# Memory attention and mLSTM numerators: from fp32 matrix products to three rounded products of split operands

## The chip, the cores and the metric

The kernel runs on one core of a Trainium2 chip. The metric is the device time of one execution in microseconds, the median of several runs. A core has TensorE (PE, matrix products; its weight loads are shown apart as PEld), VectorE (DVE), ScalarE (ACT), GpSimd (POOL) and SyncE (SP, which here issues the weight transfers).

## What is computed

A decoder trunk of two layers on 256 tokens of width 1024. Each layer is a half-step SwiGLU feed-forward (hidden width 2816), a token mixer beside four heads of attention to a memory of 256 rows, and a second half-step feed-forward. The mixer of layer 0 (mixer A) is an mLSTM with four heads, that of layer 1 (mixer B) banded attention with sixteen heads. All inputs are float32. What the change touches:

```
mem_kv = rms_norm(mem, mem_norm_g) @ mem_w_kv            # keys: first 512 columns, values: last 512
# memory_heads, per layer and head (dimension 128):
q = rms_norm(xq, q_norm_g); k = rms_norm(mem_k, k_norm_g)
s = einsum('bthd,bmhd->bhtm', q, k) * M_HD ** -0.5
p = softmax(s);  o = einsum('bhtm,bmhd->bthd', p, mem_v)
# mLSTM, per head (q, k of 128, v of 256):
s = einsum('bhjd,bhsd->bhjs', qc, kc) * exp(log_d - m_t[..., None])
num = einsum('bhjs,bhsv->bhjv', s, vc) + (part of the earlier chunks)
den = sum(s) + ...;  h = num / max(|den|, exp(-m_t))
```

The kernel computes the mLSTM over all 256 tokens at once: a lower triangle of score tiles d (128x128 tiles: three per head) times v. A column of ones next to v's 256 columns gives the denominators.

## The kernel before

**Split operands.** Nearly all products are "rounded": a float32 matrix is split into a high half, rounded to float32r, and a low half, the rest. `mm3` adds three products of the halves (low x high, high x high, high x low). Weights come in by DMA (`wr`), ScalarE writes the high half (`wh`), VectorE the low half (`wl`). Activations are split likewise (`xh`, `xl`; in the general pool tiles named `u`). `split_plain` splits as it stands, `split_gain` multiplies by a column first: both take one ScalarE and one VectorE instruction. In a product one side moves through TensorE and one stands in it; the profile names the moving one first. In the feed-forwards and output projections the weights stand; in the projections by rows (memory keys and values, memory queries, mLSTM v, all of mixer B's input) the weights move and the activations stand.

**Products that are fp32.** `mmf` issues a plain float32 product, which the profile shows as two MATMUL records. It is used for the memory scores (`kT` moving, query `qT` standing), the memory values (`pT` moving, `vM` standing), the mLSTM scores and the mLSTM numerators (`v` moving with 257 columns, score tiles `d` standing). Transpositions (with the identity `con`) and mixer B's banded attention are fp32 as well.

**Side chains.** The main program issues the large projections. Each head is a chain of steps started beside it: for a memory head queries, scores, softmax, transposition of p, values; for an mLSTM head scores, numerators, normalisation, transposition. The steps are `cross_spawn` and its inner `queries` and `head`, and `scores` and `numerators` in `mixer_a`.

**Order.** The kernel is first recorded, then `plan` orders all instructions on each engine with a table of durations: TensorE takes the next run of the main program or a side run whose operands are ready; VectorE and ScalarE take the instruction that is due first; SyncE issues transfers in the recorded sequence. A rule with `HOLD` holds back a lone side run for up to 2 us while the previous product was a rounded one, so that side runs come together. Tiles come from pools with a fixed number of buffers: `up` (31 units of 2 KB a partition), `tp` (7 of the same size, named `t`), `vp` (2), `whp` and `wlp` (8 each), `cp` (small columns).

**Addresses.** In the built program the activation halves (pools `xhp`, `xlp`, `up`) begin at byte 448 modulo 512 of a partition, and the weight halves (`whp`, `wlp`) and `tp` at 0. `kT` and `vM` are at 448, `v` at 448 and 480.

Of the kernel before, what the change touches and what calls it, by code (L numbers as in the profile page):

```python
# [10 lines left out]
F32 = mybir.dt.float32  # L11
# [8 lines left out]
P = 128  # L20
# [153 lines left out]
class Slot:  # L174
    def __init__(self, pool, tag, number, shape, dt, name):
        self.key, self.pool, self.number, self.uses, self.made = (pool.name, tag), pool, number, [], None
        self.args = (shape, dt, tag, name)

    def real(self):
        if self.made is None:  # L180
# [144 lines left out]
def plan(rec):  # L325
# [11 lines left out]
    tiles_of, touched = [[] for _ in ops], [[] for _ in ops]  # L337
    for slots in rec.slots.values():
        over = []
        for s in slots:  # L340
            s.users = sorted({u[0].n for u in s.uses})
            s.first, s.left, s.end, s.free_from, s.psum = s.users[0], len(s.users), 0.0, 0.0, s.key[1] == "bank"
# [100 lines left out]
    while remaining:  # L443
        found = []
        if now:
            found.append((free["tensor"], now[0], None))
        else:
            t0 = free["tensor"]
            head = main[at["main"]] if at["main"] < len(main) else None
            r0 = ready(head[0]) if head else None  # L450
            if head and tiles_of[head[0].n] and side and len(places[tiles_of[head[0].n][0].key]) <= SPARE:
                r0 = None
            best, there = None, 0
            for run in side[:24]:
                r = run_ready(run)
                if r is not None:
                    r += MARGIN
                    there += r <= t0
                    if best is None or max(r, t0) < best[0]:
                        best = (max(r, t0), run, r)  # L460
            if best and last_kind and there < 2 and t0 - best[2] < HOLD and r0 is not None and r0 <= t0:
                best = None
            if best and (r0 is None or best[0] <= max(r0, t0)):
                found.append((best[0], best[1][0], best[1]))
            elif r0 is not None:
                found.append((max(r0, t0), head[0], head))
# [68 lines left out]
def tile_trunk(ctx: ExitStack, nc, a, out):  # L535
# [15 lines left out]
    xhp = pool("xhp", 4)  # L551
    xlp = pool("xlp", 4)
    up = pool("up", 31)
    vp = pool("vp", 2)
    wrp = pool("wrp", 5)
    whp = pool("whp", 8)
    wlp = pool("wlp", 8)
    tp = pool("tp", 7)
    sp = pool("sp", 2)
    ap1 = pool("ap1", 1)  # L560
    gp = pool("gp", 1)
# [10 lines left out]
    def unit(dt):  # L572
        return mk(up, [P, 2, T], dt, "u")

    def tmp():
        return mk(tp, [P, 2, T], F32, "t")

    def col():
        return mk(cp, [P, 16], F32, "col")
# [267 lines left out]
        return halves(ps)  # L847


    kT = [mk(cst, [P, 2, T], F32, f"kT{i}") for i in range(2)]  # L850
    vM = mk(cst, [P, 2, 512], F32, "vM")
    x0 = Norm(G_F1)

    def memory():
# [20 lines left out]
        norm = Norm(G_MEM, rows=False)  # L875

        def keys(gi, kr):
            nc.scalar.copy(kT[gi], turn(kr))
            return
            yield  # L880

# [13 lines left out]
        def finish(raw):  # L895
            for c2 in range(4):
                norm.square(memT[c2], c2 == 0)
                yield 2.0
            norm.fold()
            yield LAT['mnorm']  # L900
            yield from norm.chain()
            yield LAT['mrest']
            for h in range(2):
                nc.vector.tensor_scalar(vM[:, h], vM[:, h], norm.rc[:, h:h + 1], None, op0=ALU.mult)
            hsc = head_scales(norm.zc, P, False)
            for i in range(2):
# [5 lines left out]
        raw = [unit(F32) for _ in range(2)]  # L912
        for gi in range(4):
            gr = Group(wkv, gi * 256, mh, ml, rows=True)
            wts = [wcols(wkv, 768, kh) for kh in range(2)] if gi == 3 else wfirst if gi == 0 else [None] * 2
            if gi == 3:
                for c2 in range(4):
                    x0.put(xT[c2], False)
            for kh in range(2):
                if gi == 0 and kh == 0:  # L920
                    yield from gr.first_part(wts[0])
                else:
                    yield from gr.part(kh, wts[kh])
            dst = raw[gi] if gi < 2 else vM[:, :, (gi - 2) * 256:(gi - 1) * 256]
            wv.spawn(late(dst, gr), LAT['raw'])
# [108 lines left out]
    def cross_spawn(gr, gi, layer, hsc, ys):  # L1034
# [4 lines left out]

        def queries():  # L1040
            ps = turn(qn)
            qT = unit(F32)
            act(qT, ps, AF.Copy, scale=gqk[:, layer:layer + 1])
            cell.append(qT)
            for m in range(2):
                wv.spawn(head(m), LAT['cross_s'] + LAT['cross_m'] * m)
            return
            yield

        def head(m):  # L1050
            hd, qT = gi * 2 + m, cell[0]
            hi, lo = ys.tiles(4 + gi)
            s = mo()
            for h in range(2):
                mmf(s[:, h * T:(h + 1) * T], qT[:, m, h * P:(h + 1) * P], kT[gi][:, m], T)
            sv = halves(s)
            c = col()
            nc.vector.tensor_reduce(out=c[:, 0:2], in_=sv, axis=AX.X, op=ALU.max, negate=True)
# [9 lines left out]
            for mc in range(2):  # L1068
                for h in range(2):
                    transpose(tps[:, mc * T + h * P:mc * T + (h + 1) * P], p[:, h, mc * P:(mc + 1) * P])  # L1070
            pT = tmp()
            nc.scalar.copy(pT, halves(tps))
            yield LAT['cross_o']
            o = mo()
            for mc in range(2):
                mmf(o[:, :T], vM[:, mc, hd * P:(hd + 1) * P], pT[:, mc], T, mc == 0, mc == 1)
            split_plain(o[:, :T], hi[:, m], lo[:, m])
            ys.done.add(8 + hd)

# [38 lines left out]
    def mixer_a(x, nxt):  # L1118
# [112 lines left out]

        def numerators(hd, v):
            d = sd[hd]
            nps = [mo(), mo()]
            mmf(nps[0][:, :257], d[:, :P], v[:, 0, :257], 257)
            mmf(nps[1][:, :257], d[:, P:T], v[:, 0, :257], 257, True, False)
            mmf(nps[1][:, :257], d[:, T:384], v[:, 1, :257], 257, False, True)
            c, junk = col(), tmp()
            for h in range(2):
                nc.vector.tensor_copy(c[:, h:h + 1], nps[h][:, T:T + 1])  # L1240
# [35 lines left out]
    rope_s = mk(cst, [P, 2, 2, ROT], F32, "rope_s")  # L1276

    def rope_tables():
        w16 = [mk(sp, [P, 2, 8], F32, f"rope{i}") for i in range(5)]
        ang, k, r, sn, cs = w16  # L1280
        posf = col()
        nc.vector.tensor_copy(posf[:, 0:2], posi)
# [216 lines left out]
```

## Time and profile before

| | |
|---|---|
| three runs | 998.93 us (median), 998.85 to 999.69 |
| the profiled execution | 998.74 us |
| its span | 997.0 us |
| granted TensorE clock | 1.0 |
| TensorE, VectorE, ScalarE busy | 99%, 67%, 53% |
| instructions | 20571, 8560 of them MATMUL records |

The span is divided as follows (us from its start): memory stage to about 31, first feed-forward to about 237, mixer A to about 324, two feed-forwards to about 709, mixer B to about 813, last feed-forward to the end. Every operation is issued by one helper, so all have one line (237); groups are told apart by the names of their tiles.

### The profile page before, as it was taken

Reading aid. Unit: us, or ns where it says so; the run is one execution under the profiler, and the core shown is the slowest. Engines: PE = TensorE matmul, PEld = TensorE weight load, DVE = VectorE, ACT = ScalarE, POOL = GpSimd, SP = SyncE. Lnnn points to the kernel's source line nnn. Section 1 sums busy time; section 2 is a strip of 40 time slices with the busy share of each in tenths; the row PEclk is TensorE's granted clock in tenths of the full one; section 3 lists DMA queues with packets and bytes.
Section 4 is the critical chain, followed back from the end, with each engine's and each line's share of the span. In section 5 each row is a group of like instructions: output and inputs, shape, how many; then the busy total and the mean of one; then the engine's idle time right before and its main releaser. Section 6 shows DMA issues by size and latency. Waiting matters only on the chain.

```text
span 997.0 us, 20571 instructions
## 1 busy us (share of the span) xinstructions
PE 990.9 (99%) x8560; PEld 974.1 (98%) x8560; DVE 664.6 (67%) x1080; ACT 532.8 (53%) x779; POOL 27.0 (3%) x27
## 2 busy tenths in 40 slices
PE   9999999999999999999999999999999999999998
PEld 7999999999999999999999999999998899999998
DVE  6986665578756686666567766656677777666552
ACT  7764545446746554444455544445578765544440
POOL 0020000000001000000000000000113000000000
PEclk9999999999999999999999999999999999999999
DMA  9966665667544566665666666556633437665550
GB/s 323 299 200 193 195 189 179 198 171 206 155 149 148 170 212 192 195 200 173 190 202 204 192 196 198 176 187 200 184 106 123 132 106 235 195 199 187 181 169 22
DMA packets 173204, 182.70 MB, mean 183 GB/s; under 512 B 7124, under 2 KB 168328, under 8 KB 173112
## 3 DMA queue, kind: packets, MB, share of 16 engines
q1 hardware_dynamic: 171872, 179.60, 58.6%
q10 hardware_dynamic: 1016, 1.58, 0.5%
q8 instruction: 67, 1.10, 0.5%
q0 software_dynamic: 224, 0.22, 0.2%
q14 instruction: 25, 0.20, 0.1%
HBM read 180.32 MB, written 1.05 MB: 182 GB/s over the span
## 4 chain that ended last, share of the span: by engine, by line
PE 98%; DMA 1%; SPq 0%; DVE 0%; ACT 0%; issue 0%
PE bank L237 98%; DMA wr<-in_mem_w_kv_dram 1%; SPq L237 0%; DVE wl L237 0%; ACT wh L237 0%; DVE t L237 0%
## 5 line engine op out<-in xcount | busy, mean ns | idle before, releaser
L237 DVE TENSOR_TENSOR wl<-wr,wh 128x1024 fp32r<-128x1024 f32 (+1 forms) x349 | 414.8, 1191 | 265.2 <-ACT wh L237 263.6
L237 ACT CAST wh<-wr 128x1024 fp32r<-128x1024 f32 (+1 forms) x349 | 357.8, 1027 | 390.2 <-PE bank L237 372.9
L237 PE MATMUL bank<-xh,wh 128*128 128x256 f32 x1544 | 427.0, 277 | 0.0
L237 PE MATMUL bank<-xh,wl 128*128 128x256 f32 x1544 | 426.7, 276 | 0.0
L237 PE MATMUL bank<-xl,wh 128*128 128x256 f32 x1544 | 426.5, 276 | 0.0
L237 PE MATMUL bank<-u,wh 128*128 128x256 f32 x1792 | 307.3, 277 | 0.0
L237 PEld LDWEIGHTS bank<-xh,wh 128*128 128x128 f32 x1544 | 290.0, 188 | 0.1
L237 PEld LDWEIGHTS bank<-xh,wl 128*128 128x128 f32 x1544 | 290.0, 188 | 0.0
L237 PEld LDWEIGHTS bank<-xl,wh 128*128 128x128 f32 x1544 | 289.9, 188 | 0.1
L237 PEld LDWEIGHTS bank<-u,wh 128*128 128x128 f32 x1792 | 270.0, 188 | 1.4 <-issue 1.4
L237 PE MATMUL bank<-u,wl 128*128 128x256 f32 x896 | 248.1, 277 | 0.0
L237 PEld LDWEIGHTS bank<-u,wl 128*128 128x128 f32 x896 | 168.3, 188 | 0.5 <-issue 0.5
L237 PE MATMUL bank<-wh,xh 128*128 128x256 f32 x208 | 58.6, 282 | 0.0
L237 PE MATMUL bank<-wh,xl 128*128 128x256 f32 x208 | 58.6, 282 | 0.0
L237 PE MATMUL bank<-wl,xh 128*128 128x256 f32 x208 | 58.3, 280 | 0.0
L237 DVE TENSOR_TENSOR t<-bank,rb 128x256 f32<-128x256 f32 x88 | 36.6, 421 | 11.1 <-PE bank L237 9.1
L237 DVE TENSOR_TENSOR u<-t,u 128x512 fp32r<-128x512 f32 (+1 forms) x59 | 40.4, 685 | 0.3
L237 PEld LDWEIGHTS bank<-wh,xh 128*128 128x128 f32 x208 | 39.1, 188 | 0.1
L237 PEld LDWEIGHTS bank<-wh,xl 128*128 128x128 f32 x208 | 39.0, 188 | 0.1
L237 PEld LDWEIGHTS bank<-wl,xh 128*128 128x128 f32 x208 | 39.0, 188 | 0.1
L237 DVE TENSOR_TENSOR t<-t,bank 128x256 f32<-128x256 f32 x88 | 32.8, 414 | 1.1 <-ACT t L237 1.1
L237 POOL TENSOR_TENSOR col<-col,mhalf 128x4 f32<-128x4 f32 (+2 forms) x15 | 21.8, 1456 | 294.1 <-DVE col L237 294.1
(134 smaller groups left out, 581.5 us busy)
## 6 DMA issues: line engine op xcount, KB each, us to landing
wr<-in_ffn_w_in_dram SPq DMA_DIRECT2D x176, 512.0 KB, 4.4
wr<-in_ffn_w_out_dram SPq DMA_DIRECT2D x80, 512.0 KB, 4.2
wr<-in_a_w_in_dram SPq DMA_DIRECT2D x28, 512.0 KB, 3.7
wr<-in_b_w_in_dram SPq DMA_DIRECT2D x14, 512.0 KB, 4.5
wr<-in_a_w_out_dram SPq DMA_DIRECT2D x12, 512.0 KB, 3.3
wr<-in_b_w_out_dram SPq DMA_DIRECT2D x12, 512.0 KB, 3.5
wr<-in_ffn_w_out_dram SPq DMA_DIRECT2D x16, 256.0 KB, 2.8
wr<-in_mem_w_kv_dram SPq DMA_DIRECT2D x7, 512.0 KB, 7.7
```

The lines of the kernel that those rows point to most:

```text
L237: getattr(getattr(nc, op.engine), op.kind)(*map(real, op.args), **{k: real(x) for k, x in op.kw.items()})
```

## The change

The products of the memory heads and of the numerators become three rounded products each. Keys and values of the memory are kept as high and low halves: 2 x 2 tiles `kT`, two tiles `vM`. The values go through two more `u` units first and are scaled and split by `split_gain`. The query becomes two `t` tiles, the transposed probabilities two `u` tiles, the mLSTM score tiles two `t` tiles, and v two tiles with 258 columns (the ones column and a second one; zeros in the low half). Scores keep kT moving and the query standing; values keep the probabilities moving and vM standing; numerators keep v moving and the score tiles standing.

Gaps in the constants and between the two v pools set addresses: `kT` at 448, `vM` at 0, the v halves at 448 and 480, all modulo 512; the pools behind keep the offsets that they had modulo 512. `tp` grows to 8, the rope tables' small tiles come from `cp`, and the area for GpSimd's transfer descriptors is halved. In `plan` the `HOLD` rule no longer holds a side run that begins with a rounded product. The mLSTM scores, the transpositions and mixer B's banded attention stay as they were.

```diff
-            if best and last_kind and there < 2 and t0 - best[2] < HOLD and r0 is not None and r0 <= t0:
+            if best and last_kind and not best[1][0].rounded and there < 2 and t0 - best[2] < HOLD and r0 is not None and r0 <= t0:
...
-    vp = pool("vp", 2)
+    vhp = pool("vhp", 2)
+    gap = pool("gap", 1)
+    vlp = pool("vlp", 2)
...
-    tp = pool("tp", 7)
+    tp = pool("tp", 8)
...
-    kT = [mk(cst, [P, 2, T], F32, f"kT{i}") for i in range(2)]
-    vM = mk(cst, [P, 2, 512], F32, "vM")
+    kT = [[mk(cst, [P, 2, T], F32R, f"kT{i}{j}") for j in range(2)] for i in range(2)]
+    mk(cst, [P, 16], F32, "gap1")
+    vM = [mk(cst, [P, 2, 512], F32R, f"vM{j}") for j in range(2)]
+    mk(cst, [P, 112], F32, "gap2")
+    mk(gap, [P, 112], F32, "gap")
...
         def keys(gi, kr):
-            nc.scalar.copy(kT[gi], turn(kr))
+            split_plain(turn(kr), *kT[gi])
...
-            for h in range(2):
-                nc.vector.tensor_scalar(vM[:, h], vM[:, h], norm.rc[:, h:h + 1], None, op0=ALU.mult)
+            for i in range(2):
+                for h in range(2):
+                    split_gain(raw[2 + i][:, h], norm.rc[:, h:h + 1],
+                               *(v[:, h, i * 256:(i + 1) * 256] for v in vM))
...
         def queries():
             ps = turn(qn)
-            qT = unit(F32)
-            act(qT, ps, AF.Copy, scale=gqk[:, layer:layer + 1])
-            cell.append(qT)
+            cell.extend((tmp(F32R), tmp(F32R)))
+            split_gain(ps, gqk[:, layer:layer + 1], *cell)
...
             for h in range(2):
-                mmf(s[:, h * T:(h + 1) * T], qT[:, m, h * P:(h + 1) * P], kT[gi][:, m], T)
+                qh, ql = (q[:, m, h * P:(h + 1) * P] for q in cell)
+                mm3(s[:, h * T:(h + 1) * T], qh, ql, kT[gi][0][:, m], kT[gi][1][:, m], True, True)
...
-            pT = tmp()
-            nc.scalar.copy(pT, halves(tps))
+            ph, pl = unit(F32R), unit(F32R)
+            split_plain(halves(tps), ph, pl)
...
             for mc in range(2):
-                mmf(o[:, :T], vM[:, mc, hd * P:(hd + 1) * P], pT[:, mc], T, mc == 0, mc == 1)
+                vh, vl = (v[:, mc, hd * P:(hd + 1) * P] for v in vM)
+                mm3(o[:, :T], vh, vl, ph[:, mc], pl[:, mc], mc == 0, mc == 1)
...
         def numerators(hd, v):
             d = sd[hd]
+            dh, dl = (x4.rearrange("p a b -> p (a b)") for x4 in (tmp(F32R), tmp(F32R)))
+            split_plain(d[:, :384], dh[:, :384], dl[:, :384])
+            yield 0.0
             nps = [mo(), mo()]
-            mmf(nps[0][:, :257], d[:, :P], v[:, 0, :257], 257)
-            mmf(nps[1][:, :257], d[:, P:T], v[:, 0, :257], 257, True, False)
-            mmf(nps[1][:, :257], d[:, T:384], v[:, 1, :257], 257, False, True)
+            for h, ds, c in ((0, slice(0, P), 0), (1, slice(P, T), 0), (1, slice(T, 384), 1)):
+                mm3(nps[h][:, :T + 2], dh[:, ds], dl[:, ds], v[0][:, c], v[1][:, c], c == 0, h == c)
...
-            v = mk(vp, [P, 2, T + 2], F32, "v")
-            nc.vector.memset(v[:, :, T:T + 1], 1.0)
+            v = [mk(vhp, [P, 2, T + 2], F32R, "vh"), mk(vlp, [P, 2, T + 2], F32R, "vl")]
+            for x2, one in zip(v, (1.0, 0.0)):
+                nc.vector.memset(x2[:, :, T:].bitcast(F32), one)
             for h in range(2):
-                act(v[:, h, :T], gr.ps[:, h], AF.Copy, scale=x.rc[:, h:h + 1])
+                split_gain(gr.ps[:, h], x.rc[:, h:h + 1], *(x2[:, h, :T] for x2 in v))
```

On TensorE, where the first mLSTM numerators stand in mixer A (u is the score tile, bank the result; the neighbours are the projection that runs on), before:

```order
L237 MATMUL bank_3759<-wl_3565,xh_2656 128x256
L237 MATMUL bank_3814<-v_3491,u_3280 128x257
L237 MATMUL bank_3818<-v_3491,u_3280 128x257 x2
L237 MATMUL bank_3759<-wh_3547,xl_2850 128x256
L237 MATMUL bank_3759<-wh_3547,xh_2837 128x256
```

and after (t are the halves of the score tile; the first three of nine such products):

```order
L238 MATMUL bank_3837<-wh_3579,xh_2859 128x256
L238 MATMUL bank_3887<-vh_3527,t_3649 128x258
L238 MATMUL bank_3887<-vh_3527,t_3638 128x258
L238 MATMUL bank_3887<-vl_3530,t_3638 128x258
L238 MATMUL bank_3891<-vh_3527,t_3649 128x258
```

Three fp32 products became nine rounded ones at the same place among the rows of the projection; line 237 of the helper is line 238 in the changed kernel.

More of the change, by code (lines that the diff above doesn't have):

```diff
@@ L177, in __init__ @@
         self.args = (shape, dt, tag, name)
+        self.psum = tag == "bank"
     def real(self):
@@ L339, in plan @@
         over = []
-        for s in slots:
+        for s in (s for s in slots if s.uses):
             s.users = sorted({u[0].n for u in s.uses})
-            s.first, s.left, s.end, s.free_from, s.psum = s.users[0], len(s.users), 0.0, 0.0, s.key[1] == "bank"
+            s.first, s.left, s.end, s.free_from = s.users[0], len(s.users), 0.0, 0.0
             tiles_of[s.first].append(s)
@@ L573, in unit, with tmp @@
         return mk(up, [P, 2, T], dt, "u")
-    def tmp():
-        return mk(tp, [P, 2, T], F32, "t")
+    def tmp(dt=F32):
+        return mk(tp, [P, 2, T], dt, "t")
     def col():
@@ L910, in finish @@
                 wv.spawn(keys(i, kr), LAT['mkeys'])
-        raw = [unit(F32) for _ in range(2)]
+        raw = [unit(F32) for _ in range(4)]
         for gi in range(4):
@@ L923, in memory @@
                     yield from gr.part(kh, wts[kh])
-            dst = raw[gi] if gi < 2 else vM[:, :, (gi - 2) * 256:(gi - 1) * 256]
-            wv.spawn(late(dst, gr), LAT['raw'])
+            wv.spawn(late(raw[gi], gr), LAT['raw'])
             if gi == 1:
@@ L1050, in head @@
         def head(m):
-            hd, qT = gi * 2 + m, cell[0]
+            hd = gi * 2 + m
             hi, lo = ys.tiles(4 + gi)
@@ L1278, in rope_tables @@
     def rope_tables():
-        w16 = [mk(sp, [P, 2, 8], F32, f"rope{i}") for i in range(5)]
+        w16 = [col().rearrange("p (a b) -> p a b", a=2) for _ in range(5)]
         ang, k, r, sn, cs = w16
@@ L1479 @@
     from concourse.bass_utils import run_bass_kernel_spmd as _run
-    nc = _bacc.Bacc("TRN2", target_bir_lowering=False, num_devices=1)
+    nc = _bacc.Bacc("TRN2", target_bir_lowering=False, num_devices=1, dynamic_dma_scratch_size=8192)
     v = {n: np.ascontiguousarray(x) for n, x in inputs.items()}
```

## The prediction

> **What bounds the kernel now.** I read the page's busy times and its chain first, then the list of waits, then the instructions of TensorE in order of time at the places the change touches, then the groups by shape for prices. Page, busy times and the chain that ended last:
>
> ```profile
> PE 990.9 (99%) x8560; PEld 974.1 (98%) x8560; DVE 664.6 (67%) x1080; ACT 532.8 (53%) x779; POOL 27.0 (3%) x27
> ...
> PE bank L237 98%; DMA wr<-in_mem_w_kv_dram 1%; SPq L237 0%; DVE wl L237 0%; ACT wh L237 0%; DVE t L237 0%
> ```
>
> The time is TensorE's instruction stream. A busy TensorE could still be a waiting one, so the list of waits (who, for whom, total us, times, longest):
>
> ```profile
> ACT wh L237 <- PE bank L237: 372.9, 269, 3.0
> ...
> PE bank L237 <- DVE t L237: 1.2, 1, 1.2
> ...
> PE bank L237 <- DVE wl L237: 0.8, 1, 0.8
> ...
> PE bank L237 <- ACT wh L237: 0.3, 1, 0.3
> ```
>
> TensorE waits 2.3 us in all; ScalarE waits 373 us for TensorE to give weight buffers back, so weights lie split well ahead. What shortens TensorE's stream shortens the kernel, and a new wait of TensorE lengthens it one for one.
>
> **The products that go.** Groups by shape (mean ns is the pipelined length, not the spacing), then TensorE in time, where spacing is read from starts; an fp32 product is two MATMUL records:
>
> ```profile
> L237 PE MATMUL bank<-t,vM 128*128 128x256 f32 x32 | 8.3, 382 | 0.0
> L237 PE MATMUL bank<-kT,u 128*128 128x256 f32 x32 | 7.8, 380 | 0.0
> ...
> L237 PE MATMUL bank<-v,u 128*128 128x257 f32 x24 | 5.9, 380 | 0.0
> ```
>
> ```profile
> 257.10 1.89 PE L237 MATMUL bank<-kT,u 128*128 128x256 f32 x8
> 258.83 0.60 PE L237 MATMUL bank<-con,u 128*128 128x128 f32 x4
> 259.27 1.03 PE L237 MATMUL bank<-t,vM 128*128 128x256 f32 x4
> 259.94 0.47 PE L237 MATMUL bank<-xh,wh 128*128 128x256 f32 x1
> 260.25 0.28 PE L237 MATMUL bank<-xl,wh 128*128 128x256 f32 x1
> ```
>
> ```profile
> 299.56 1.47 PE L237 MATMUL bank<-v,u 128*128 128x257 f32 x6
> 300.86 0.60 PE L237 MATMUL bank<-con,t 128*128 128x128 f32 x4
> ```
>
> Four products with kT take 258.83 - 257.10 = 1.73 us, 0.433 each; three with v take 1.30, 0.433 each. The change removes 16 with kT, 16 with vM, 12 with v: 44 x 0.433 = 19.05 us.
>
> In their place stand 44 x 3 = 132 rounded products. One row of a table by stretch inside a feed-forward, and a slow stretch from its first to its last row (89 steps):
>
> ```profile
> 327.00:500.00 173.00, 173.00 (x1529) 173.00 (x1528) 113.66 (x151) 86.51 (x107) 0.00 (x0) 1.00 0.62 190
> ```
>
> ```profile
> 31.24 0.28 PE L237 MATMUL bank<-xh,wl 128*128 128x256 f32 x1
> ...
> 41.72 0.28 PE L237 MATMUL bank<-xl,wh 128*128 128x256 f32 x1
> 41.84 0.40 PE L237 MATMUL bank<-u,onesr 128*128 128x256 f32 x2
> ...
> 42.20 0.28 PE L237 MATMUL bank<-xh,wh 128*128 128x256 f32 x1
> ```
>
> Fast: 173.0 us over 1529 less the two or three that only reach over the edges, 0.1133. Slow: 10.48 us over 89, 0.1178. So 132 cost 14.96 us fast or 15.55 slow, and the saving is 4.1 or 3.5. Most new products stand among fast ones; I take **-4.0**. The 36 of the numerators move 258 columns instead of 256, which at the same rate adds 0.03 us in all.
> [...]
>
> **Seams.** From 259.27 to 260.25 stand two vM products (0.87) and one rounded (0.113): 0.98, as observed, so a change between fp32 and rounded products is nearly free here. The rows' last digit allows 0.01 at each end; twenty groups go, which makes 0.4 at most, and transpositions next to many of them stay fp32. I take **-0.2** (0 to -0.4).
>
> How the order moves: TensorE in mixer A, scores of a memory head of the second group (con is the identity, so those are transpositions; bank takes the result). Before:
>
> ```order
> L237 MATMUL bank_3303<-xh_2837,wl_3074 128x256
> L237 MATMUL bank_3391<-con_101,u_3329 128x128 x4
> L237 MATMUL bank_3398<-kT_26_115,u_3375 128x256 x2
> L237 MATMUL bank_3405<-kT_26_115,u_3375 128x256 x2
> L237 MATMUL bank_3410<-con_101,u_3339 128x128 x4
> L237 MATMUL bank_3420<-t_3400,vM_116 128x256 x2
> ```
>
> After (t is now the split query, 122 and 123 the high and low key):
>
> ```order
> L238 MATMUL bank_3427<-xl_2333,wh_3115 128x256
> L238 MATMUL bank_3434<-con_107,u_3353 128x128 x4
> L238 MATMUL bank_3441<-kT_27_122,t_3414 128x256
> L238 MATMUL bank_3441<-kT_27_122,t_3396 128x256
> L238 MATMUL bank_3441<-kT_28_123,t_3396 128x256
> ```
>
> An fp32 pair became threes of rounded products, and the value product that followed directly now runs among projection rows.
>
> **The cadence.** The slow cadence is a stretch, not an operand: 89 products with weights standing ran slow from 31.24, right after products with weights moving, and the ones products ended it. Groups with weights moving against weights standing:
>
> ```profile
> L237 PE MATMUL bank<-xh,wh 128*128 128x256 f32 x1544 | 427.0, 277 | 0.0
> ...
> L237 PE MATMUL bank<-wh,xh 128*128 128x256 f32 x208 | 58.6, 282 | 0.0
> L237 PE MATMUL bank<-wh,xl 128*128 128x256 f32 x208 | 58.6, 282 | 0.0
> L237 PE MATMUL bank<-wl,xh 128*128 128x256 f32 x208 | 58.3, 280 | 0.0
> ```
>
> The 624 with weights moving are mostly slow (5 ns longer, as the slow stretch's 4.5). All of them at the fast cadence would give 624 x 0.0045 = 2.8 us; a longer slow stretch would cost. In the built program's layout the new side products have moving and standing operands at the feed-forward's byte offsets (448 and 0 modulo 512; the second v buffer 480), where the old ones had 448 and 448 or 0 and 448, so fewer of them should start a slow stretch; transpositions and the banded attention, which stay, still do. Nearer the low end: **-0.8** (from +0.5 to -2.8).
> [...]
>
> **VectorE and ScalarE.** Prices, and both mixers' stretches (columns TensorE, weight loads, VectorE, ScalarE, GpSimd):
>
> ```profile
> L237 DVE TENSOR_TENSOR u<-t,u 128x512 fp32r<-128x512 f32 x44 | 30.1, 684 | 0.0
> ...
> L237 DVE SCALAR_TENSOR_TENSOR xl<-u,gcol,xh 128x256 fp32r<-128x256 f32 x48 | 20.7, 476 | 0.0
> ...
> L237 DVE TENSOR_TENSOR u<-u,bank 128x384 f32<-128x384 f32 x4 | 2.2, 555 | 0.5 <-PE bank L237 0.2
> ```
>
> ```profile
> 236.00:326.00 90.00, 90.00 (x725) 87.87 (x724) 59.81 (x119) 57.36 (x107) 5.75 (x6) 1.00 0.52 158
> 708.00:816.00 108.00, 108.00 (x895) 98.01 (x894) 79.02 (x219) 77.83 (x183) 14.70 (x8) 1.00 0.40 127
> ```
>
> Low halves on VectorE: 8 x 0.68 for probabilities, 4 x 0.7 for queries, 4 x 0.56 for score tiles, 8 x 0.48 for v: 14.3 us on 138.8 busy of 198, so 77%. The high halves replace copies of the same size, but for four more of 384 columns. In the memory stage the low halves of keys and values cost VectorE at most 2 x 0.68 + 4 x 0.48 = 3.3 us more. Weights are split far ahead, so **0** on the path; if that cover were gone, it would be the third rival. SP issues the same transfers in the same sequence; GpSimd's rows are the same. The smaller descriptor area and the rope tiles touch only GpSimd's six small loads and small VectorE work: 0.
>
> **A new wait.** TensorE at the end of mixer B: the last head's value product (t, u), its split on ScalarE and VectorE, and output-projection products that go on meanwhile:
>
> ```profile
> 805.58 0.87 PE L237 MATMUL bank<-t,u 128*64 128x256 f32 x8
> 806.38 0.50 PE L237 MATMUL bank<-u,wh 128*128 128x256 f32 x2
> 806.49 0.37 ACT L237 CAST u<-bank 128x256 fp32r<-128x256 f32 x1 [1.29 <-PE bank L237]
> 806.72 0.28 PE L237 MATMUL bank<-u,wl 128*128 128x256 f32 x1
> ...
> 806.90 0.42 DVE L237 TENSOR_TENSOR u<-bank,u 128x256 fp32r<-128x256 f32 x1 [0.43 <-ACT u L237]
> ```
>
> High half at 806.86, low half at 807.32. Before, on TensorE, fourteen products stand between that head and the first that reads its result (wl_9989); the rows at that end:
>
> ```order
> L237 MATMUL bank_9710<-u_10258,wl_9927 128x256
> L237 MATMUL bank_9710<-u_10258,wh_9910 128x256
> L237 MATMUL bank_9710<-u_10264,wh_9910 128x256
> L237 MATMUL bank_9710<-u_10258,wl_9989 128x256
> L237 MATMUL bank_9710<-u_10258,wh_9965 128x256
> ```
>
> After, the reader (wl_10167) stands right behind the head:
>
> ```order
> L238 MATMUL bank_10475<-t_10442,u_9219 64x128
> L238 MATMUL bank_10475<-t_10449,u_9219 64x128
> L238 MATMUL bank_9885<-u_10455,wl_10167 128x256
> L238 MATMUL bank_9885<-u_10455,wh_10151 128x256
> L238 MATMUL bank_9885<-u_10463,wh_10151 128x256
> ```
>
> The third reader needs the low half: it would start at 806.72 and can at about 807.37, so **+0.65**; on ScalarE a weight split (1.05 us) stands ahead of this one, which can add to it. Behind the waiting product all of TensorE is queued. Elsewhere the order brings TensorE closer to its operands, as with the ones products of the first feed-forward, which stand 18 products (2.0 us) earlier; I add **+0.35**. Range for all waits 0 to +3.
>
> **Sum.** -4.0 - 0.2 - 0.8 + 0 + 1.0 = -4.0 us. The profiled execution took 998.74 us (span 997.0), 0.19 below the median of 998.93; the sum gives 994.7 on it and **994.9** against the median.
>
> **Rivals.**
> - *The offsets work fully*: rows with weights moving run at 0.1133 (-2.8) and no wait but the 0.65: 998.9 - 4.1 - 0.4 - 2.8 + 0.65 = 992.3. For it: the slow stretch ended as soon as the side changed at 41.84. Against: fp32 transpositions remain in every such stretch. 0.13.
> [...]
> - *Longer chains eat the saving*: each of 20 groups has a VectorE step of 0.68 us more ahead of it. If five find nothing to cover it, that is 3.4 us more in place of the 0.35: 998.0. It ends the gain within 0.2% from about three uncovered groups. Against: TensorE's waits of 2.3 us today and VectorE's spare 23%. 0.14.
> - *A slow stretch catches a feed-forward* (the other side): the head at the end of mixer B leaves TensorE slow and nothing in the last feed-forward but one pair of ones products interrupts it. This stretch:
>
> ```profile
> 830.00:990.00 160.00, 160.00 (x1415) 160.00 (x1414) 92.00 (x119) 67.71 (x77) 0.00 (x0) 1.00 0.55 169
> ```
>
> 1415 x 0.0045 = 6.4 us: 1001.3. From some 900 slow products on (4.0 / 0.0045) the gain is gone. Against: at 41.84 the ones products ended one. 0.07.
>
> **How the numbers follow.** Forecast 0.66 (993.4 to 996.7). A measurement here can tell about 0.2%, 2 us, from no change: faster is below 996.9. Forecast and first rival give 0.79, and a third of the 0.14 may still end faster; I say 0.8 faster, 0.13 same, 0.07 slower. The range reaches from the first rival to the third, 992.2 to 998.0, leaving out the slow feed-forward and the edges.
>
> **What would show it.** In the changed profile: kT, vM and v without fp32 products, and 132 rounded ones at 0.1133 to 0.1178; weights-moving groups a little below 282 ns; a wait of TensorE of 0.5 to 1 us for VectorE or ScalarE u ahead of the last feed-forward. I am wrong if 20 side groups show waits, if a feed-forward takes 0.1178 a product, or if rounded products of this size are dearer than in the feed-forward.

## The result, and the profile after

The changed kernel takes 1004.29 us (median of 15, 1003.32 to 1013.23) where the kernel before took 999.28 in the same series. It is slower in every execution. Its times fall in two groups: of 20 in two series 11 lie between 1003.3 and 1005.1 and 9 between 1011.2 and 1013.2. The ratio to the kernel before is 1.0078 (95%: 1.0062 to 1.0094); it mixes the two groups, which by their medians in this series (1003.81 and 1011.60) stand at 1.0045 and 1.0123. The profiled execution is one of the upper group (1013.23, span 1011.4).

The page after, busy times and chain; TensorE's stream bounds the kernel as before, only longer:

```profile
PE 1003.5 (99%) x8604; PEld 989.4 (98%) x8604; DVE 677.6 (67%) x1112; ACT 534.1 (53%) x787; POOL 27.4 (3%) x27
...
PE bank L238 98%; DMA wr<-in_mem_w_kv_dram 1%; SPq L238 0%; DVE wl L238 0%; ACT wh L238 0%; DVE t L238 0%; ACT u L238 0%
```

The same two stretches inside feed-forwards as before the change (TensorE first, with its count; the granted clock is the 1.00):

```profile
327.00:500.00 173.00, 173.00 (x1471) 173.00 (x1470) 109.23 (x146) 82.44 (x102) 0.00 (x0) 1.00 0.60 184
830.00:990.00 160.00, 160.00 (x1361) 160.00 (x1361) 96.44 (x126) 70.80 (x82) 0.00 (x0) 1.00 0.57 178
```

1471 products where 1529 fitted, 1361 where 1415 did: 0.1177 us a product, the slow cadence, at full clock and without a gap. (The cadence is the distance from the start of one product to the start of the next.) None of these products was changed. In time order on TensorE (con is the identity; u and wh, wl belong to mixer A's output projection), a group of transpositions that leaves the fast cadence behind it and the next group, which leaves the slow one:

```profile
316.75 0.60 PE L238 MATMUL bank<-con,t 128*128 128x128 f32 x4
317.10 0.48 PE L238 MATMUL bank<-u,wh 128*128 128x256 f32 x2
...
317.78 0.28 PE L238 MATMUL bank<-u,wl 128*128 128x256 f32 x1
317.89 0.39 PE L238 MATMUL bank<-u,wh 128*128 128x256 f32 x2
318.12 0.28 PE L238 MATMUL bank<-u,wl 128*128 128x256 f32 x1
...
322.54 0.60 PE L238 MATMUL bank<-con,t 128*128 128x128 f32 x4
322.90 0.36 PE L238 MATMUL bank<-u,wl 128*128 128x256 f32 x1
323.10 0.40 PE L238 MATMUL bank<-u,wh 128*128 128x256 f32 x2
323.33 0.28 PE L238 MATMUL bank<-u,wl 128*128 128x256 f32 x1
323.45 0.40 PE L238 MATMUL bank<-u,wh 128*128 128x256 f32 x2
```

From 317.78 a triple, the three products of one split pair, takes 0.34; from 323.10 it takes 0.35 (0.117 + 2 x 0.118), and so it goes on for 219 us, through one pair of ones products at 356 (the two sums of a norm, against the constant tile onesr) and up to the next:

```profile
542.40 0.28 PE L238 MATMUL bank<-xh,wh 128*128 128x256 f32 x1
542.53 0.40 PE L238 MATMUL bank<-u,onesr 128*128 128x256 f32 x2
542.77 0.28 PE L238 MATMUL bank<-xl,wh 128*128 128x256 f32 x1
```

The second slow stretch begins at the end of mixer B, at the wait that the prediction had named, and lasts to the end of the kernel:

```profile
813.66 0.87 PE L238 MATMUL bank<-t,u 128*64 128x256 f32 x8
815.00 0.39 PE L238 MATMUL bank<-u,wl 128*128 128x256 f32 x1 [0.47 <-ACT u L238]
815.22 0.62 PE L238 MATMUL bank<-u,wh 128*128 128x256 f32 x2
815.68 0.28 PE L238 MATMUL bank<-u,wl 128*128 128x256 f32 x1
```

Where the time went, from the starts of the first product of each stage (profiled executions, us):

| stage | before | after | difference |
|---|---|---|---|
| to the first feed-forward | 31.24 | 34.36 | +3.12 (first weights later; +0.54 in another execution) |
| first feed-forward | 181.31 | 180.91 | -0.40 |
| mixer A | 133.04 | 130.68 | -2.36 |
| two feed-forwards | 359.49 | 366.93 | +7.44 |
| mixer B | 108.11 | 107.75 | -0.36 |
| last feed-forward to the end | 183.81 | 190.77 | +6.96 |

The stages are cut here at their first product (before: 31.24, 212.55, 345.59, 705.08, 813.19), so the first feed-forward ends at 212.55 and not at about 237 as said ahead of the prediction, and mixer A takes in its own projections with weights standing. The mixers, where the change is, became shorter. The feed-forwards behind them, which it does not touch, pay about 14 us.

### The profile page after: what moved, and what is told of

Its sections match the earlier page's. It is cut to its first block, busy times and chain, and to the rows that moved or that the text cites. A ratio compares the mean times of both kernels' runs of the same rounds, so it can differ in the third digit from the quotient of the medians.

```text
span 1011.4 us, 20709 instructions
## 1 busy us (share of the span) xinstructions
PE 1003.5 (99%) x8604; PEld 989.4 (98%) x8604; DVE 677.6 (67%) x1112; ACT 534.1 (53%) x787; POOL 27.4 (3%) x27
## 4 chain that ended last, share of the span: by engine, by line
PE 98%; DMA 1%; SPq 0%; DVE 0%; ACT 0%; issue 0%
PE bank L238 98%; DMA wr<-in_mem_w_kv_dram 1%; SPq L238 0%; DVE wl L238 0%; ACT wh L238 0%; DVE t L238 0%; ACT u L238 0%
## 5 line engine op out<-in xcount | busy, mean ns | idle before, releaser
L238 ACT CAST wh<-wr 128x1024 fp32r<-128x1024 f32 (+1 forms) x349 | 357.4, 1026 | 409.0 <-PE bank L238 386.1
L238 PE MATMUL bank<-u,wh 128*128 128x256 f32 x1792 | 313.6, 279 | 0.0
L238 PEld LDWEIGHTS bank<-u,wh 128*128 128x128 f32 x1792 | 273.2, 189 | 0.7 <-issue 0.5
```

The source lines that it names most:

```text
L238: getattr(getattr(nc, op.engine), op.kind)(*map(real, op.args), **{k: real(x) for k, x in op.kw.items()})
```

## The experiments

A seam is here the place where TensorE comes back to a long stretch of rounded products from something else: transpositions, an fp32 product, ones products, products with the sides exchanged, a wait. The main theory (A): a product's cadence is a state, fast or slow, that the seam ahead of a stretch sets and that then holds. Against it: the new products or their waits are dear in themselves (B, C), or offsets and seams do nothing.

**The changed kernel again.** No edit.

> The changed kernel again, unchanged. The profile taken first (1011.4 us) shows both second halves of the work after a mixer slow: from 323.1 to 542.6 us, and from 815.7 us to the end, at 0.1178 us a rounded product instead of 0.1133. Theory A (the slow cadence is a state that a seam sets off by chance of a few ns, and that holds until the next seam): times fall in two groups, near 1003.5 and near 1011.5, and a profile near 1003.5 has one of the two feed-forward stretches fast (about 1940 x 4.45 ns = 8.6 us or 1630 x 4.45 ns = 7.2 us less). Theory B (the new operands themselves are dear wherever they stand, some 8 us in all): every execution shows the same slow rows, and the 132 new products carry the difference. Theory C (new waits of TensorE): rows of waits of TensorE sum to over 5 us.

Five times: 1003.46, 1003.55, 1011.6, 1011.85, 1011.89. The profile (1011.85) has both stretches slow again, at the same places. B falls, since the 132 new products take 15.8 us from start to start in both profiles, within 1 us of their price, and 8 us more are not among them; C falls, since TensorE's waits for other engines sum to 3.5 us there, for 2.3 before. An execution of the lower group was not caught in a profile; 8.2 us is about what the first stretch alone makes (1862 x 0.0045 = 8.4).

**A sweep of offsets and seams.** TensorE alone; its core:

```diff
+    for mv in range(8):
+        for st in range(8):
+            for seam in seams:
+                seam()
+                products(mv, st, RUN)
```

> Not the computation: TensorE alone runs 384 short series of 20 rounded products of 256 columns (weights 128x128 fp32r standing, fp32r moving), for each of 8 byte offsets (steps of 64 modulo 512) of the moving and of the standing side, each after one of six seams: 4 transpositions, 3 transpositions, 1 fp32 product, 2 fp32 products, 2 rounded products, 6 rounded products with the sides exchanged. The outputs are not the reference's. Theory A1 (a state that depends on offsets and on the seam): for some pairs of offsets every series is at 0.1133 us a product whatever the seam, for others some series are at 0.1133 and others at 0.1178 for all 20 products. Theory A2 (a state without offsets): both spacings occur at every pair of offsets, by the seam alone. [...]

The six series at moving 448 and standing 0, the kernel's own offsets. L43 are transpositions, L47 fp32 products (two records each), L52 the products with sides exchanged, L39 the rounded series; the x42 is a series, two seam products and the next series:

```profile
801.21 2.53 PE L39 MATMUL bank<-X,W 128*128 128x256 f32 x20
803.58 0.49 PE L43 MATMUL bank<-con,raw 128*128 128x128 f32 x3
803.82 2.53 PE L39 MATMUL bank<-X,W 128*128 128x256 f32 x20
806.19 0.59 PE L47 MATMUL bank<-raw 128*128 128x256 f32 x2
806.43 2.71 PE L39 MATMUL bank<-X,W 128*128 128x256 f32 x20
808.97 1.02 PE L47 MATMUL bank<-raw 128*128 128x256 f32 x4
809.65 5.23 PE L39 MATMUL bank<-X,W 128*128 128x256 f32 x42
814.72 0.87 PE L52 MATMUL bank<-W,X 128*128 128x256 f32 x6
815.43 2.45 PE L39 MATMUL bank<-X,W 128*128 128x256 f32 x20
```

A series of 20 from its start to the next seam takes 2.37 after transpositions (0.1133 apart inside) and 2.54 after one fp32 product (0.1178 inside; the first step of it is 0.1 longer after fp32). So one pair of offsets has both cadences, by the seam: A1. By the difference of the offsets (moving less standing, modulo 256) all series fall in classes, with the odd steps of 32 from the finer sweep below (means from the seventh step of a series on):

| difference | us a product | fast series |
|---|---|---|
| 0 | 0.1195 to 0.1200 | 0 of 125 |
| 32 / 224 | 0.1164 to 0.1178 / 0.1180 to 0.1185 | 0 of 32 each |
| 64 | 0.1133 or 0.1178 | 13 of 128 |
| 96 / 160 | 0.1196 to 0.1204 / 0.1172 to 0.1200 | 0 of 32 each |
| 128 | 0.1183 to 0.1202 | 0 of 127 |
| 192 | 0.1133 or 0.1178 | 76 of 128 |

Only 64 and 192 know the fast cadence, and neither keeps it by itself. Nor does a kind of seam fix it: at 192, behind one fp32 product 6 of the 16 series of this sweep were fast, behind four transpositions 9 of 16. The kernel's products with weights standing have 192 (448 - 0), those with weights moving 64; it fits that the latter are slow more often (420 of 592 in series of 12 or more in the kernel before). That offsets and seams do nothing falls: with nothing but these changed, a product takes 0.1133 to 0.1204. What in TensorE makes an offset cost was not shown.

**Seams at the entries of the feed-forwards.** An fp32 pair, a control of two rounded products, and four transpositions, as the first work of the two feed-forwards that were slow; the fp32 pair with its loop, then what stands in its place:

```diff
+            if gi == 0 and seam:
+                for i in range(2):
+                    mmf(ps[0][:, :T], x.xT[0][:, 0, i * P:(i + 1) * P], x.xT[0][:, 1], T, i == 0, i == 1)
...
+                    nc.tensor.matmul(ps[0][:, :T], x.xh[0][:, 0, i * P:(i + 1) * P], x.xh[0][:, 1], start=i == 0, stop=i == 1,
+                                     skip_group_check=True)
...
+                for i in range(4):
+                    transpose(ps[0][:, i % 4 * P:(i % 4 + 1) * P], x.xT[0][:, i // 2, i % 2 * P:(i % 2 + 1) * P])
```

> The changed kernel, with two fp32 products of 256 columns put as the first TensorE work of the feed-forward after mixer A and of the one after mixer B (they write a bank that the next product starts anew; the result is not touched). In the profile of the changed kernel (1011.9) those feed-forwards begin slow at 344.5 and 819.2 us; until 541.3 us and the end they hold about 1670 and 1620 products at 0.1178. Theory A (a state that a seam sets, and an fp32 pair of this size sets it to fast, as in every one of the sweep's series with moving 448 and standing 0 and ahead of all five groups of products with weights standing behind such pairs in the changed kernel): both run at 0.1133, 7.5 + 7.3 us less, 4 x 0.433 more: 1011.6 - 14.8 + 1.7 = 998.5, and the two groups of times (1003.5 and 1011.6) become one. Theory B (the new products are dear in themselves, or their waits are): 1.7 us more than now, 1005.2 and 1013.3.

> The control to the fp32 pair: at the same two places two rounded products of 256 columns with one tile on both sides. In the sweep two rounded products ahead of a series with moving 448 and standing 0 left it slow. Theory A (the kind of seam decides): still slow, two groups of times, 0.24 to 0.5 us above 1003.5 and 1011.6. Rival A' (any interruption throws the state anew, by chance): it falls in some executions to 996 to 1004.

> At the same two places a group of four fp32 transpositions of 128 columns (0.36 us with its seam 0.45). Theory A: in the changed kernel transpositions ahead of products with weights standing left the fast state in 10 groups of 13, the slow one in 3 (one of these is the group at 321.5 us that begins the long stretch); so likely fast here too, 1011.6 - 14.8 + 0.9 = 997.7, with a chance that one of the two stays slow (1005). Theory B: 1004.4 and 1012.5.

Measured: fp32 pair 998.69 (ratio 0.9998, 0.9989 to 1.0008), rounded pair 1004.98 (1.0059, 1.0044 to 1.0074), transpositions 997.34 (0.9984, 0.9974 to 0.9993); no second group in any. The two stretches, for the rounded pair and for the transpositions:

```profile
327.00:500.00 173.00, 173.00 (x1519) 1.00 0.61 189
830.00:990.00 160.00, 160.00 (x1360) 1.00 0.54 167
```

```profile
327.00:500.00 173.00, 173.00 (x1523) 1.00 0.61 189
830.00:990.00 160.00, 160.00 (x1414) 1.00 0.54 167
```

The transpositions took 6 and 14 us out of the two groups of times, where B had 1 us more. The control left the last feed-forward slow (1360), and there it made it slow: ahead of the pair a triple takes 0.34, behind it 0.35 (xh is one tile on both sides):

```profile
811.71 0.39 PE L238 MATMUL bank<-u,wh 128*128 128x256 f32 x2
...
812.05 0.39 PE L238 MATMUL bank<-u,wh 128*128 128x256 f32 x2
812.28 0.40 PE L238 MATMUL bank<-xh 128*128 128x256 f32 x2
812.52 0.28 PE L238 MATMUL bank<-xh,wl 128*128 128x256 f32 x1
...
812.87 0.28 PE L238 MATMUL bank<-xh,wl 128*128 128x256 f32 x1
```

In the first feed-forward the slow cadence went through the control, and the ones products at 355 ended it this time, so the four executions make one group of times, 1.4 above the lower one of the changed kernel, where I had expected two. In the run with four transpositions the cadence ahead of the second seam was fast already, so only the first of them turned slow into fast. The fp32 pair met its number but not its story: in the first feed-forward it turned slow into fast,

```profile
343.54 1.03 PE L238 MATMUL bank<-u 128*128 128x256 f32 x4
344.21 0.47 PE L238 MATMUL bank<-xh,wl 128*128 128x256 f32 x1
```

and from 344.87 on products stand 0.113 apart; in the last one the cadence was already fast and the pair turned it slow, until the ones products 8 us later. So one kind of seam gave both outcomes in one execution; it does not fix the cadence.

**Finer offsets and more seams.** The same program with steps of 32 bytes, and 126 series of 24 at the kernel's own two pairs of offsets, behind 21 kinds of seams (not 18).

> Not the computation: TensorE alone again, series of 20 products for byte offsets in steps of 32 modulo 256 of both sides after four seams, and then, at moving 448 and standing 0 and with the sides exchanged, series of 24 after 18 kinds of seams in three orders. The outputs are not the reference's. The first sweep showed by the difference of the offsets (moving less standing, modulo 256): 0 always 0.1200, 128 always 0.1187, 64 and 192 either 0.1133 or 0.1178 by the seam. Theory A1: the odd steps of 32 bytes give values of their own, and if one of them is 0.1133 after every seam, that is a layout without the slow state. Rival: only steps of 64 matter, an odd step reads like its neighbour, and no offset is free of it. Seams: fp32 pairs and six or more products with the sides exchanged leave the fast state at moving 448 and standing 0 in every order; single fp32 products and two rounded ones leave the slow one or whatever was there.

The odd steps have values of their own (table above), none as fast as 0.1133: A1 without the free layout. Seams at 448 against 0: 37 of 63 series fast. One or two transpositions, five and eight: all fast; three: 2 of 3; four and six: 1 of 3 each. fp32 pairs of 256 columns 3 of 3, one or four of them 0 of 6; exchanged products 3 of 3 after three, 0 of 6 after two or four, 5 of 9 after six, nine or twelve. My second expectation, that six or more exchanged products always help, fell. With the sides exchanged 10 of 63 are fast.

**One fp32 product in the kernel before.** The sharpest test of A: nothing of the change, and the seam that left slow series.

```diff
+            if gi == 0 and seam:
+                mmf(ps[0][:, :T], x.xT[0][:, 0, :P], x.xT[0][:, 1], T)
```

> The kernel before, with none of the change, and one fp32 product of 256 columns put as the first TensorE work of the feed-forward after mixer A and of the one after mixer B (in the sweeps a single such product left moving 448 against standing 0 slow in all five series, a pair of them fast). Its own cost is 0.433 plus about 0.2 for the seam, twice: 1.3 us. Theory A (the state of the feed-forward is set by the seam ahead of it and belongs to no product of the change): both feed-forwards run at 0.1178 until a seam ends it, about 1690 and 1580 products x 0.0045 = 7.6 and 7.1 us: 999.1 + 1.3 + 14.7 = 1015; if the ones products end it in one of them, about 1008. Theory B (the new products are dear): 1000.4.

1021.33 us, ratio 1.0215 (1.0201 to 1.0229): two products of 0.433 us add 22. The first one, the spacing ahead of it 0.34 a triple and behind it 0.35, and the two stretches:

```profile
345.80 0.28 PE L237 MATMUL bank<-u,wl 128*128 128x256 f32 x1
...
346.14 0.59 PE L237 MATMUL bank<-u 128*128 128x256 f32 x2
346.38 0.47 PE L237 MATMUL bank<-xh,wl 128*128 128x256 f32 x1
346.69 0.28 PE L237 MATMUL bank<-xh,wh 128*128 128x256 f32 x1
...
347.04 0.28 PE L237 MATMUL bank<-xh,wh 128*128 128x256 f32 x1
```

```profile
327.00:500.00 173.00, 173.00 (x1476) 1.00 0.59 183
830.00:990.00 160.00, 160.00 (x1360) 1.00 0.59 185
```

It went past my 1015, because the ones products at 545 did not end the slow cadence either and the feed-forward behind them paid another 1483 x 0.0045 = 6.7: 1015 + 6.7 = 1021.7. (The 0.2 us that I had set for each seam is not in the rows: 346.69 - 346.14 = 0.55 is the fp32 product and one rounded one.)

**Two transpositions, and the halves of the change.** Two in place of four; then, with four, the numerators' or the memory heads' parts as they were before:

```diff
-                for i in range(4):
+                for i in range(2):
```

```diff
-            v = [mk(vhp, [P, 2, T + 2], F32R, "vh"), mk(vlp, [P, 2, T + 2], F32R, "vl")]
+            v = mk(vp, [P, 2, T + 2], F32, "v")
```

```diff
-    kT = [[mk(cst, [P, 2, T], F32R, f"kT{i}{j}") for j in range(2)] for i in range(2)]
-    vM = [mk(cst, [P, 2, 512], F32R, f"vM{j}") for j in range(2)]
+    kT = [mk(cst, [P, 2, T], F32, f"kT{i}") for i in range(2)]
+    vM = mk(cst, [P, 2, 512], F32, "vM")
```

> The changed kernel with two transpositions in place of four at the entries of the two feed-forwards. In the second sweep one or two transpositions left moving 448 against standing 0 fast in all six series, four in some. Theory A: both feed-forwards fast, 4 x 0.109 = 0.44 us less than with four (997.34): 996.9, below the kernel before (999.1) and the changed one (1003.5 and 1011.6). Rival (the outcome hangs on some ns of the seam's place, not on the count): one of the two feed-forwards slow in some executions, 1004.

> Half of the change: memory heads as rounded products, the numerators left in fp32 with the two v buffers of the kernel before; four transpositions at the two entries, as in the run that gave 997.34. With both feed-forwards fast the two halves can be told apart: 12 fp32 products come back, 12 x 0.433 = 5.2 us for the 4.34 us that the 36 rounded ones of 258 columns take in the changed kernel's profile: 997.34 + 0.9 = 998.2. Rival (the numerators' longer chain of splits costs more than it saves): 997.3 or below.

> The other half: numerators as rounded products, memory attention left in fp32 with kT and vM in fp32 as in the kernel before; four transpositions at the two entries. 32 fp32 products come back, 32 x 0.433 = 13.9 us for the 96 rounded ones at 0.1133 to 0.1178 (10.9 to 11.3): 997.34 + 2.6 to 3.0 = 1000. Seen from the kernel before it is 999.1 + 0.9 (seams) - 0.9 (numerators) = 999.1; the two ends differ by what the memory heads cost in waits and slow series. Above 1003: one feed-forward slow, whatever half is in.

Two transpositions at each entry: 997.00, ratio 0.9973 (0.9963 to 0.9984), faster than both kernels. 1522 and 1414 products stand in the two stretches of above. Here the cadence was 0.118 ahead of both seams and 0.1133 behind both, so each of them turned slow into fast. Memory heads alone 999.02 (0.9996, 0.9987 to 1.0005), numerators alone 1001.30 (1.0019, 1.0009 to 1.0028), each about 1 us above what was expected. Both feed-forwards run fast in both profiles; the spacing above 0.1133 in the other stretches sums to 5.4 us in the second and 4.2 in the first, where the whole change has 3.4. So each rearrangement draws new outcomes at some hundred seams, worth 1 to 2 us, and the halves can't be priced closer than that. Mixer A, with the four transpositions at its end, took 131.3 with memory heads alone, 133.5 with numerators alone and 131.0 with both (before 133.0, without transpositions): the gain there is the memory heads'.

**The clause on held side steps.** In the 997.00 kernel, TensorE around the first ones products of the first feed-forward:

```profile
40.11 0.39 PE L238 MATMUL bank<-u,onesr 128*128 128x256 f32 x1
41.41 0.39 PE L238 MATMUL bank<-u,onesr 128*128 128x256 f32 x1 [0.91 <-DVE u L238]
```

```diff
-            if best and last_kind and not best[1][0].rounded and there < 2 and t0 - best[2] < HOLD and r0 is not None and r0 <= t0:
+            if best and last_kind and there < 2 and t0 - best[2] < HOLD and r0 is not None and r0 <= t0:
```

> The changed kernel with two transpositions at the entries of the two feed-forwards (997.0 us), and the clause of the change taken back that lets rounded side steps go as soon as they are ready: they are held for company again as before. In the order the first ones products of the first feed-forward then stand behind 90 products as in the kernel before, not 72. In the profile with the clause TensorE waits there twice, 1.29 and 0.22 us between starts where 0.113 is normal: 1.29 us too much. Theory: that wait is the clause's and goes: 997.0 - 1.3 = 995.7, with both feed-forwards fast. Rival (a held step makes another late, or a feed-forward turns slow by another seam): 997 or above; 1003 with one slow.

The wait is gone, since the pair now stands behind 90 products:

```profile
42.45 0.40 PE L238 MATMUL bank<-u,onesr 128*128 128x256 f32 x2
42.70 0.28 PE L238 MATMUL bank<-xh,wl 128*128 128x256 f32 x1
```

and the time is 998.69 (0.9993, 0.9984 to 1.0002), 1.7 above and not 1.3 below. The first feed-forward took 181.3 for 182.4, as expected; mixer A took 131.8 for 130.8 and mixer B 108.5 for 107.8, and the spacing above 0.1133 outside the gaps rose from 4.1 to 5.2 us. The rival holds: the other order gave other seams. The execution of the 997.00 kernel that was profiled is also the longest of its eight (998.03); whether the others have the wait of 1.3 us is not shown.

**One offset on both sides.**

```diff
-            cell.extend((tmp(F32R), tmp(F32R)))
+            cell.extend((unit(F32R), unit(F32R)))
...
-            ph, pl = unit(F32R), unit(F32R)
+            ph, pl = tmp(F32R), tmp(F32R)
```

> The changed kernel with four transpositions at the two entries (997.34 us), and the split queries taken from the units (byte offset 448, as kT) and the split probabilities from the other pool (0, as vM): both sides of the 96 products of the memory heads stand at one offset. The sweep gives 0.1200 a product for equal offsets, whatever the seam. Theory A1: rows of these products 0.120 apart, where they are 0.1133 to 0.1178 (mean of 96 without seams 0.1153) in the run with different offsets: 96 x 0.0047 = 0.45 us, 997.8. Rival (offsets do nothing): 0.1153 and 997.3. Above 1003: a feed-forward caught by another seam.

998.23 (0.9988, 0.9978 to 0.9997), 0.9 above the run with different offsets by the medians; the ratios' intervals overlap, so the time alone does not decide. Twelve score products in a row, with one offset and then with two:

```profile
250.09 1.60 PE L238 MATMUL bank<-kT,u 128*128 128x256 f32 x12
251.52 0.28 PE L238 MATMUL bank<-xl,wh 128*128 128x256 f32 x1
```

```profile
250.28 1.52 PE L238 MATMUL bank<-kT,t 128*128 128x256 f32 x12
251.64 0.28 PE L238 MATMUL bank<-xl,wh 128*128 128x256 f32 x1
```

1.43 / 12 = 0.119 against 1.36 / 12 = 0.1133. Over all 96 products the spacings sum to 0.34 us more, a little less than the 0.45 expected: the offsets that the change gives these products are worth that much.

## Why the prediction was wrong, point by point

- **The failed step: the slow stretch.** The prediction held the right mechanism as its last rival, with the right price (0.0045 a product) and even the place, and gave it 0.07. Two things in it were wrong. Its argument against, that ones products ended such a stretch at 41.84, was one case; the runs show pairs that did not end it at 356 and 830 in the changed kernel and at 355, 545 and 838 in the kernel with one fp32 product. And it looked at one feed-forward, where three can be caught. What was treated as a small term of cadence (-0.8, at worst +0.5) came to +14.4 in the profiled execution, one of the upper group. The rows of before showed that three of the four feed-forwards began fast (the first began slow, at 31.24); they did not show what that would survive, and I took it for the normal case.
- **The products.** 44 fp32 products went and 132 rounded ones came, as said. The new ones took 15.8 us between starts against 14.96 to 15.55: the 36 of 258 columns stand 0.1205 apart, not 0.114, and about 0.4 us are first steps behind transpositions. Mixer A gave 2.36 us, mixer B 0.36, together 2.7 where the terms of products and seams had 4.2 and the wait 0.65.
- **The cadence inside the mixers.** Products with weights moving did become a little quicker, as forecast: a mean of 280, 280 and 279 ns where it was 282, 282 and 280.

```profile
L238 PE MATMUL bank<-wh,xh 128*128 128x256 f32 x208 | 58.3, 280 | 0.0
L238 PE MATMUL bank<-wh,xl 128*128 128x256 f32 x208 | 58.1, 280 | 0.0
L238 PE MATMUL bank<-wl,xh 128*128 128x256 f32 x208 | 58.0, 279 | 0.0
```

  By the starts, 172 of 592 such products in series of 12 or more were fast before and 289 of 596 after. All fast would have given 1.9 us (590 steps of 0.1165 on average), not the 2.8 that the prediction read from the mean durations. And as much was lost again elsewhere: in the repaired kernels the spacing above 0.1133 sums to 3.4 to 4.1 us where the kernel before has 3.6. This term is 0, not -0.8.
- **VectorE and ScalarE.** 0 held. VectorE rose from 664.6 to 677.6 us, and the weights' splits stay ahead: ScalarE waits 386.1 us for TensorE to give weight buffers back, where it was 372.9.
- **The new waits.** The one at the end of mixer B is there, behind 813.66. From the start of the last head's value products to the first reader of its result it is 815.00 - 813.66 = 1.34 us, where before the next product stood 806.38 - 805.58 = 0.80 behind; and the three steps behind that reader take 0.223, 0.236 and 0.221, where before they took 0.223, 0.117 and 0.117. Together that is 0.77 us where 0.65 was forecast. The ones products' wait, in the nine profiles of kernels with the new clause on held side steps, is 1.1 to 1.6 us in four, 0.5 in two, and 0.1 or none in three, the one of the changed kernel above, whose first weights came later, among them; I had 0.35 for all of these. Together 0.8 to 2.3 against 1.0.
- **The sum.** With both feed-forwards fast the change gives 997.0, less about 0.5 for the seams put in (from the first transposition to the second product behind it 345.17 - 344.83 = 0.34 where one step of 0.11 would stand, twice): 996.5 where 994.9 was forecast. That would have been within the range; without the state the forecast was 1.6 us too low. The products (-3.3 for -4.0), the cadence (0 for -0.8) and the waits (0.8 to 2.3 for 1.0) make 1.3 to 2.8 of a miss, and 1.6 lies within that; how many executions have the ones products' wait is not known, so it can't be settled closer.
- **No effect of the offsets**, for which the range of the cadence term (+0.5 to -2.8) had room, fell with the sweeps: 0.1195 to 0.1200 us a product at equal offsets, 0.1133 or 0.1178 at differences of 64 and 192.

What stays open: what in a seam decides. Groups of transpositions led to both cadences in the same program. In the twelve profiles of the kernels, series of 12 or more products with weights standing were fast behind all 74 groups of transpositions whose first step was 0.202 us or longer, and behind 25 of 46 where it was 0.200 or 0.201; behind the group at 322.54 it was 0.201. But this is no rule: in the finer sweep, at 448 against 0, 3 of the 18 series whose first step was 0.202 or longer were slow. That a stretch keeps its cadence was shown; what in TensorE keeps it was not.

## What to carry to other kernels

Where one kind of product fills hundreds of us, count products per us in every long stretch before and after a change: here a gain of 2.7 us in the mixers arrived with 14.4 us of a state that its seams set, in work that it doesn't touch. Such a stretch wants a seam of its own at its entry that has been measured to leave it fast; here two transpositions, 0.23 us each time, brought 1004 to 1012 down to 997.0. And no saving of 1 to 2 us could be read here from one arrangement, since the orders that were run differed by that much: with the feed-forwards fast, the spacing above 0.1133 still summed to 3.4 to 5.4 us.

## What the runs showed of the hardware

- Rounded products of 256 columns with weights standing (offsets 448 and 0) had two lasting cadences in these kernels, 0.1133 and 0.1178 us, at a granted clock of 1.00 and with the same operands; one stretch kept the slow one for over 3000 products (346 to 720 us in the kernel before with one fp32 product), through two pairs of ones products.
- Of the differences of moving and standing offsets tried, all steps of 32 modulo 256 bytes, only 64 and 192 had the fast one (13 and 76 of 128 series); equal offsets took 0.1195 to 0.1200 behind every seam tried (0 of 125 series fast).
- One fp32 product of 0.433 us at two places made an otherwise unchanged kernel 22 us slower.
